# Two pool places fewer for the expert tokens, float32 pieces at the end, and another way to the last norm

## The chip, the cores and the metric

The kernel runs on one core of a Trainium2 chip. TensorE (PE), VectorE (DVE), ScalarE (ACT), GpSimd (POOL) and SyncE (SP) run their own instruction queues; weights come from HBM by DMA. The metric is the device time of one launch in microseconds (us); lower is better.

## The reference

Two layers act on 256 tokens of width 1024, all in float32. In each, two mixers (windowed attention and a gated delta rule) are merged and added, and a channel mixer follows: a dense SwiGLU in layer 0, eight experts with the top two per token in layer 1. After each half comes a layer norm. The part that the change touches:

```
def moe_swiglu(x, router_w, w_gate, w_up, w_down):
    logits = x @ router_w
    top_val, top_idx = lax.top_k(logits, TOP_K)
    top_w = softmax(top_val)
    gates = sum(one_hot(top_idx, 8) * top_w)        # (tokens, experts)
    y = 0
    for e in range(8):
        y += gates[:, e] * ((silu(x @ w_gate[e]) * (x @ w_up[e])) @ w_down[e])
    return y                                        # w_gate, w_up: 1024 x 3584; w_down: 3584 x 1024
x = layer_norm(alpha * x + moe_swiglu(x, ...), ln2_g, ln2_b)
```

## The kernel before, in words

**Splitting.** Float32 products are built from halves: `hi` is a rounded copy of a value and `lo` the rest, and x·w is taken as hi·hi + hi·lo + lo·hi, three matmuls per 128 rows of depth.

**The stream of weights.** Every weight piece is 128 partitions x 1024 float32 (512 KB) and comes by one DMA on SP's queue (L145) into a tile `raw`. `Stream.advance` splits it: ACT casts `raw` to `whi` (L165), DVE subtracts to get `wlo` (L167). TensorE then uses the pair (`use`) and gives it back (`retire`). Two caps, set in the code by `caps(raw, spl)`, say how many pieces the program splits ahead of TensorE and how many more it loads ahead of these. Pieces marked "plain" are used in float32 as they lie in `raw`, with no cast and no subtraction.

**The pool.** `raw`, `whi`, `wlo`, and the experts' tokens come from one pool with a single tag (`k4`): 36 places of 4 KB per partition, given out in a ring. A tile that needs a place waits until the last reader of the tile that had it before is done. So a long-lived tile in the ring makes the ring shorter for all the others.

**The experts.** `moe` (L1593) runs over the eight experts, ranked by how many tokens they have, in eight stages, i = 0 to 7. Four stages (i = 1, 3, 5, 7) are "narrow": 64 slots, with hi and lo side by side as the 128 columns of the stationary operand, so two matmuls per 128 rows of depth (`packed`, L1543 and L1544). The others are "wide": 128 slots, three matmuls in gate and up (`gemm`, L473 to L475), and plain float32 down pieces (`unsplit`, L1557). A stage has seven chunks of 512 hidden columns; each chunk is four gate pieces (`mg`), four up pieces (`mu`) and four down pieces of the rank before (`oe`, `md` in the code). The hidden values pass ACT and DVE (`mgs`, L1455 to L1467), are transposed by TensorE (`ht`, L1481) and copied back as `htp` or `htn`. After a rank's last chunk, `scatter` scales its output into `oh` and `ol` (L1500, L1501), multiplies by the placement matrix (`sc`, L1507, L1508) and adds to `x` (L1511).

**The gather.** `route` (from L1260) keeps the tokens as `xnh` and `xnl`, hi and lo, two of each: four places of the pool to the end of the kernel. `gather(i)` builds the tokens of the next two ranks (`xe` wide, `xen` narrow) with four matmuls (L1394) in each of eight steps. It starts in the third chunk of an even i.

**The order.** The big matmuls are a main line; `tick` runs background chains (hidden, scatter, gather) a step at a time between them, and `lag(n)` keeps a chain back for n steps so that TensorE doesn't reach an instruction before its input is ready. `as_written` then fixes the order of PE, DVE and ACT as the program wrote it.

**The end.** The last rank's down pieces run one half of the output columns after the other (f = 0, then f = 1), seven chunks of two pieces each, all split. Then `overflow` (an If that all engines pass, L1649; not taken here), two DMAs on SP that spread the norm's g and b to all partitions (`ln_params`, L1134), and `last_norm`: statistics, then per half of 512 columns an ACT scaling, a DVE product and an addition on DVE or POOL (L1634 to L1636).

Of the kernel before, what the change touches and what calls it, by code (L numbers as in the profile page):

```python
# [187 lines left out]
class Kern:  # L188
# [234 lines left out]
    def plan(self):  # L423
# [18 lines left out]
        def add(nm, r, c, j):  # L442
            W.add((nm, r, c, j), [piece(r, i) for i in moe_pieces(nm, c, j)], 512, nm == "md" and self.plain(r))
        for i, r in enumerate(RANKS):
# [10 lines left out]

    def plain(self, r):

        return r not in NARROW

# [799 lines left out]
    def route(self):  # L1259
# [19 lines left out]
        sel = self.small([P, 2, 8], "sel", 1, BF16)  # L1279
        self.xn = [[], []]  # L1280
        for t in range(2):
            lg = yield from self.narrow(rp, 8, "lg", t)
            nc.vector.max(mx[:, t], lg)
            nc.vector.max_index(mi[:, t], mx[:, t], lg)
            nc.vector.tensor_copy(ix[:, t], mi[:, t, :2])
            nc.vector.tensor_scalar(first[:, t], io8, ix[:, t, 0:1], None, op0=OP.is_equal)
            nc.vector.scalar_tensor_tensor(sel[:, t], io8, ix[:, t, 1:2], first[:, t], op0=OP.is_equal, op1=OP.add)
            yield
            hi = self.k4([P, D], F32R, name="xnh")
            lo = self.k4([P, D], F32R, name="xnl")  # L1290
            nc.scalar.copy(hi, self.x[t])
            nc.vector.tensor_tensor(lo, self.x[t], f32(hi), op=OP.subtract)
            self.xn[0].append(hi)
            self.xn[1].append(lo)
        ps = self.bg("rank")
# [79 lines left out]
    def gather(self, i):  # L1375
# [13 lines left out]
        for d in range(8):  # L1389
            yield from self.take()  # L1390
            ps = self.bg("xe")
            for j in range(2):
                for t in range(2):
                    nc.tensor.matmul(ps[:, j * n:(j + 1) * n], lhsT=self.xn[j][t][:, d * P:(d + 1) * P],  # L1394
                                     rhs=self.Pt[i][:, t].rearrange("p e c -> p (e c)")[:, c0:c1],
                                     start=(t == 0), stop=(t == 1))
# [96 lines left out]
    def scatter(self, e, f, oe):  # L1493
# [7 lines left out]
        nc.vector.scalar_tensor_tensor(lo, oe, gs, f32(hi), op0=OP.mult, op1=OP.subtract)  # L1501
        self.flags.add(("oh", e, f))
        yield
        for t in range(2):
# [10 lines left out]
    def down(self, r, c, fs=(0, 1)):  # L1515
# [10 lines left out]
        for f in fs:  # L1526
            keys, ends = [(("md", r, c, f), 0)], dict(first=(c == 0), last=(c == 6))
            if r in NARROW:
                yield from self.packed(keys, self.oe[f], lambda k: ht[:, k], **ends)
            else:  # L1530
                yield from self.unsplit(keys, self.oe[f], lambda k: ht[:, k], **ends)
            if c == 6:
                self.add_chain(self.scatter(r, f, self.oe[f]), ("scat", r, f), 1)
# [59 lines left out]
    def moe(self):  # L1593
        nc = self.nc
        self.Pt, self.xe, self.PT, self.ht = {}, {}, {}, {}
        self.taken = False
        self.add_chain(self.route(), ("route",), 1)
        self.dense()
        first = len(self.traced())
        for i, r in enumerate(RANKS):  # L1600
            self.add_chain(self.slots(r), ("slots", r), 1)
            for c in range(0 if i else 1, 7):
                if i % 2 == 0 and c == 2 and i < NE - 1:
                    self.add_chain(self.gather(i // 2 + 1), ("gather", i // 2 + 1), 1)
                if c == 0 and i % 2 == 1:
                    self.finish([("gather", i // 2 + 1)])
                res = {}

                def go(nm):
# [4 lines left out]
                if i:  # L1614
                    self.run(self.down(RANKS[i - 1], c))
        for f in range(2):
            for c in range(7):
                self.run(self.down(RANKS[-1], c, (f,)))
        self.finish([("scat", r, f) for r in range(NE) for f in range(2)])
        self.as_written(first)  # L1620
        self.overflow()
        g2, b2 = self.ln_params(2, 1, nc.sync)
        self.last_norm(g2, b2)

    def last_norm(self, g, b):
        nc = self.nc
        mv = [self.norm_stats(t, LN_EPS) for t in range(2)]
        for t in range(2):
            x = self.x[t]
            nb = self.small([P, 1], "nb", 2)  # L1630
            nc.vector.scalar_tensor_tensor(nb, mv[t][:, 0:1], -1.0, mv[t][:, 3:4], op0=OP.mult, op1=OP.mult)
            for h in range(2):
                s = slice(h * 512, (h + 1) * 512)
                nc.scalar.activation(x[:, s], x[:, s], AF.Identity, bias=nb, scale=mv[t][:, 3:4])  # L1634
                nc.vector.tensor_tensor(x[:, s], x[:, s], g[:, s], op=OP.mult)  # L1635
                (nc.vector if h else nc.gpsimd).tensor_tensor(x[:, s], x[:, s], b[:, s], op=OP.add)  # L1636
                nc.sync.dma_start(self.out[0, t * P:(t + 1) * P, s], x[:, s])

    def overflow(self):
# [9 lines left out]
        with tc.If(n > 0):  # L1649
            with tc.For_i(0, NE, 1) as e:  # L1650
# [16 lines left out]
                for d in range(8):  # L1667
                    ps = self.bg("xe")
                    for j in range(2):
                        for t in range(2):  # L1670
                            nc.tensor.matmul(ps[:, :P], lhsT=f32(self.xn[j][t])[:, d * P:(d + 1) * P], rhs=p2[:, t],
                                             start=(j == 0 and t == 0), stop=(j == 1 and t == 1))
                    nc.vector.tensor_copy(xe[:, d], ps[:, :P])
# [43 lines left out]
    def build(self):  # L1717
# [8 lines left out]
        self.CAP_MOE0 = (12, 5)  # L1726
        self.CAP_MOE = (14, 5)
        self.LAG = 9
        with ExitStack() as es:
# [55 lines left out]
```

## Time and profile before

| | |
|---|---|
| median of 3 runs | 1896.44 us (1896.32 to 1897.02) |
| the profiled execution | 1896.58 us, span 1894.8 us |
| PE busy | 1844.7 us, 97% of the span |
| DVE busy | 1459.6 us, 77% |
| ACT busy | 1164.2 us, 61% |
| split subtractions on DVE (L167) | 838, mean 1215 ns |
| split casts on ACT (L165) | 838, mean 1047 ns |
| DMA | 513.50 MB, mean 271 GB/s, 400 and more in many slices of the expert part |

The expert part lies between about 950 and 1878 us. In 40 slices of the span PE is at nine tenths or more in nearly all. A matmul group's busy time is modelled with a pipelined end, so that neighbours overlap: the distance of two starts is the better price. "Idle" in brackets behind a row is the time for which the engine stood before it, and what released it.

### The profile page before, as it was taken

To read this page: it belongs to the slowest core of one execution; us is meant where nothing else is said; L and a number is where in the kernel's file an instruction comes from. 1 tells how busy PE (TensorE), PEld (TensorE's weight loads), DVE (VectorE), ACT (ScalarE), POOL (GpSimd) and SP (SyncE) were. 2 spreads that over 40 slices of the span, in tenths; PEclk is the share of its full clock that TensorE was granted. 3 is DMA by queue.
4 is the path that set the end of the run, shared out by engine and by line. 5 is a ranking of instruction groups with operands and counts; after the bars stand their busy time and mean duration, and the time that the engine had idled before them with its cause. 6 is when DMAs were issued, how large, how long until landed. Compare 5 with 4: busy or idle time off the path is not lost. (4 is left out here: it accounts for less than half of the span.)

```text
span 1894.8 us, 27869 instructions
## 1 busy us (share of the span) xinstructions
PE 1844.7 (97%) x9279; PEld 1466.0 (77%) x9279; DVE 1459.6 (77%) x2147; ACT 1164.2 (61%) x1710; POOL 163.0 (9%) x221
## 2 busy tenths in 40 slices
PE   8999999999999999999999999999999999999995
PEld 7998888888889998888878766886678766787663
DVE  7888666675556887757588878998788977989777
ACT  6664555454444754545357767786678866787673
POOL 2113202000001212201220000000000000000000
PEclk9999999999999999999999999999999999999997
DMA  9445343674655445444749999999999999999992
GB/s 322 140 147 179 134 150 115 203 242 147 196 200 191 142 137 189 135 147 145 252 159 335 384 409 408 366 395 391 410 400 365 402 394 409 396 372 409 409 409 107
DMA packets 154374, 513.50 MB, mean 271 GB/s; under 512 B 26320, under 2 KB 28592, under 8 KB 154224
## 3 DMA queue, kind: packets, MB, share of 16 engines
q1 hardware_dynamic: 151984, 504.10, 72.1%
q0 software_dynamic: 2240, 7.56, 1.2%
q8 instruction: 75, 1.23, 0.3%
q14 instruction: 75, 0.61, 0.1%
HBM read 506.09 MB, written 5.51 MB: 270 GB/s over the span
## 5 line engine op out<-in xcount | busy, mean ns | idle before, releaser
L167 DVE TENSOR_TENSOR wlo<-raw,whi 128x1024 fp32r<-128x1024 f32 (+1 forms) x838 | 997.3, 1215 | 219.2 <-ACT whi L165 175.2
L165 ACT CAST whi<-raw 128x1024 fp32r<-128x1024 f32 x838 | 849.7, 1047 | 238.0 <-PE oe L1557 63.6
L1557 PE MATMUL oe<-raw,htp 128*128 128x512 f32 x448 | 197.5, 592 | 0.0
L1557 PEld LDWEIGHTS oe<-raw,htp 128*128 128x128 f32 x448 | 84.7, 190 | 94.6 <-issue 91.9
L627 PE MATMUL qb<-xhl,whi 128*128 128x256 f32 x384 | 110.4, 288 | 0.0
L632 PE MATMUL qb<-xhl,wlo 128*128 128x256 f32 x384 | 108.9, 283 | 0.6 <-DVE wlo L167 0.6
L630 PE MATMUL qb<-xhl,whi 128*128 128x256 f32 x384 | 108.5, 283 | 0.0
L473 PE MATMUL at<-whi,xhl 128*128 128x512 f32 x256 | 106.8, 417 | 0.0
L475 PE MATMUL at<-whi,xhl 128*128 128x512 f32 x256 | 101.2, 395 | 0.0
L474 PE MATMUL at<-wlo,xhl 128*128 128x512 f32 x256 | 100.8, 394 | 0.0
L1543 PE MATMUL mg<-whi,xen 128*128 128x512 f32 x224 | 97.4, 435 | 0.0
L1115 POOL TENSOR_TENSOR bnmv<-bnmv,mhalf 128x1 f32<-128x1 f32 x8 | 7.0, 871 | 1006.6 <-DVE bnmv L1114 1006.6
L1543 PE MATMUL mu<-whi,xen 128*128 128x512 f32 x224 | 91.5, 409 | 0.0
L1544 PE MATMUL oe<-wlo,htn 128*128 128x512 f32 x224 | 89.6, 400 | 0.9 <-DVE wlo L167 0.9
L1543 PE MATMUL oe<-whi,htn 128*128 128x512 f32 x224 | 89.6, 400 | 0.0
L1544 PE MATMUL mu<-wlo,xen 128*128 128x512 f32 x224 | 88.7, 396 | 0.0
L1544 PE MATMUL mg<-wlo,xen 128*128 128x512 f32 x224 | 87.8, 392 | 0.0
L473 PE MATMUL mg<-whi,xe 128*128 128x512 f32 x216 | 87.7, 406 | 0.0
L475 PE MATMUL mg<-whi,xe 128*128 128x512 f32 x216 | 85.2, 394 | 0.0
L473 PE MATMUL mu<-whi,xe 128*128 128x512 f32 x216 | 85.1, 394 | 0.0
L474 PE MATMUL mg<-wlo,xe 128*128 128x512 f32 x216 | 84.9, 393 | 0.0
L475 PE MATMUL mu<-whi,xe 128*128 128x512 f32 x216 | 84.3, 390 | 0.0
(456 smaller groups left out, 3817.5 us busy)
## 6 DMA issues: line engine op xcount, KB each, us to landing
raw<-in_moe SPq DMA_DIRECT2D x672, 512.0 KB
raw<-in_trunk SPq DMA_DIRECT2D x270, 512.0 KB
lx<-LT SPq DMA_DIRECT2D x8, 256.0 KB
Dm<-dx SPq DMA_DIRECT2D x8, 256.0 KB
raw<-in_trunk SPq DMA_DIRECT2D x8, 256.0 KB
lng<-in_ln_g POOLq DMA_DIRECT2D x3, 512.0 KB, 5.8
lnb<-in_ln_b POOLq DMA_DIRECT2D x3, 512.0 KB, 8.0
dx<-zero POOLq DMA_DIRECT2D x4, 256.0 KB, 5.0
```

The lines of the kernel that those rows point to most:

```text
L165: k.last_act = nc.scalar.copy(hi[:, :, :n], raw[:, :, :n])
L167: ins = (nc.gpsimd if share and a else nc.vector).tensor_tensor(lo[:, a:b, :n], r[:, :, :n], f32(hi)[:, a:b, :n], op=OP.subtract)
L473: nc.tensor.matmul(o, lhsT=xh, rhs=hi[:, kk, :n], start=st, stop=False)
L474: nc.tensor.matmul(o, lhsT=xh, rhs=lo[:, kk, :n], start=False, stop=False)
L475: mm = nc.tensor.matmul(o, lhsT=xl, rhs=hi[:, kk, :n], start=False, stop=en)
L627: nc.tensor.matmul(o, lhsT=hi[:, kk, w], rhs=self.xhl[k // 2][:, k % 2, :S], start=(k == 0 and b % 2 == 0), stop=False, skip_group_check=True)
L630: nc.tensor.matmul(o, lhsT=hi[:, kk, w], rhs=self.xhl[k // 2][:, k % 2, S:], start=False, stop=False, skip_group_check=True)
L632: self.dense_pe = nc.tensor.matmul(o, lhsT=lo[:, kk, w], rhs=self.xhl[k // 2][:, k % 2, :S], start=False, stop=(k == 7), skip_group_check= ...
L1115: nc.gpsimd.tensor_tensor(mv[:, 3:4], mv[:, 2:3], self.mhalf[:, 0:1], op=OP.pow)
L1543: nc.tensor.matmul(o, lhsT=x(k0 + kk), rhs=hi[:, kk], start=first and i == 0 and kk == 0, stop=False)
L1544: nc.tensor.matmul(o, lhsT=x(k0 + kk), rhs=lo[:, kk], start=False, stop=last and end)
L1557: nc.tensor.matmul(o, lhsT=x(k0 + kk), rhs=w[:, kk], start=first and i == 0 and kk == 0, stop=last and end)
```

## The change

1. `route` keeps the tokens once, in float32 (`xs`): two places instead of four. Each gather step casts its 128 x 256 piece to `xsh` on ACT and subtracts to `xsl` on DVE before its four matmuls. They use the tags `cth` and `cy` of another pool, three places each; two of `cy` hold the rows of the last norm to the end.
2. In the last rank's second half (f = 1) the pieces of chunks 3 to 6, eight pieces, are plain float32, used by `unsplit`.
3. The caps are (8, 5) from the last gate and up chunk on, and (6, 8) for the last down pieces.
4. The scatter of the last rank's first half is kept back six more steps.
5. `norm_rows` loads g and b early as hi and lo rows; after the If eight matmuls spread them over the partitions into PSUM. `last_norm` takes the statistics of x[0] on DVE and of x[1] on ACT, and does all scaling in DVE instructions that read PSUM.

```diff
--- before.py
+++ after.py
@@ -440,7 +440,7 @@
             return src
         def add(nm, r, c, j):
-            W.add((nm, r, c, j), [piece(r, i) for i in moe_pieces(nm, c, j)], 512, nm == "md" and self.plain(r))
+            W.add((nm, r, c, j), [piece(r, i) for i in moe_pieces(nm, c, j)], 512, nm == "md" and self.plain(r, c, j))
         for i, r in enumerate(RANKS):
             for c in range(7):
                 for nm in ("mg", "mu"):
@@ -453,9 +453,10 @@
             for c in range(7):
                 add("md", RANKS[-1], c, f)
-    def plain(self, r):
-        return r not in NARROW
+    def plain(self, r, c=0, f=0):
+        return r not in NARROW or (r == RANKS[-1] and f == 1 and c > 2)
     def gemm(self, keys, accs, x, first=True, last=True, tiles=(0, 1)):
@@ -1277,7 +1278,8 @@
         ix = self.small([P, 2, 2], "ix")
         first = self.small([P, 2, 8], "first")
         sel = self.small([P, 2, 8], "sel", 1, BF16)
-        self.xn = [[], []]
+        self.xs = [self.k4([P, 2, 512], name="xs") for _ in range(2)]
         for t in range(2):
             lg = yield from self.narrow(rp, 8, "lg", t)
             nc.vector.max(mx[:, t], lg)
@@ -1286,12 +1288,8 @@
             nc.vector.tensor_scalar(first[:, t], io8, ix[:, t, 0:1], None, op0=OP.is_equal)
             nc.vector.scalar_tensor_tensor(sel[:, t], io8, ix[:, t, 1:2], first[:, t], op0=OP.is_equal, op1=OP.add)
             yield
-            hi = self.k4([P, D], F32R, name="xnh")
-            lo = self.k4([P, D], F32R, name="xnl")
-            nc.scalar.copy(hi, self.x[t])
-            nc.vector.tensor_tensor(lo, self.x[t], f32(hi), op=OP.subtract)
-            self.xn[0].append(hi)
-            self.xn[1].append(lo)
+            for h in range(2):
+                nc.scalar.copy(self.xs[h][:, t], self.x[t][:, h * 512:(h + 1) * 512])
         ps = self.bg("rank")
         nc.tensor.matmul(ps[:, 0:8], lhsT=self.triS, rhs=sel[:, 0], start=True, stop=True)
         nc.tensor.matmul(ps[:, 8:16], lhsT=self.ones16, rhs=sel[:, 0], start=True, stop=False)
@@ -1388,10 +1386,15 @@
         n = c1 - c0
         for d in range(8):
             yield from self.take()
+            x = self.xs[d // 4][:, :, d % 4 * P:(d % 4 + 1) * P]
+            xp = [self.mp.tile([P, S], F32R, name=nm, tag=tag, bufs=3).rearrange("p (t c) -> p t c", t=2)
+                  for nm, tag in (("xsh", "cth"), ("xsl", "cy"))]
+            nc.scalar.copy(xp[0], x)
+            nc.vector.tensor_tensor(xp[1], x, f32(xp[0]), op=OP.subtract)
             ps = self.bg("xe")
             for j in range(2):
                 for t in range(2):
-                    nc.tensor.matmul(ps[:, j * n:(j + 1) * n], lhsT=self.xn[j][t][:, d * P:(d + 1) * P],
+                    nc.tensor.matmul(ps[:, j * n:(j + 1) * n], lhsT=xp[j][:, t],
                                      rhs=self.Pt[i][:, t].rearrange("p e c -> p (e c)")[:, c0:c1],
                                      start=(t == 0), stop=(t == 1))
             v = ps[:, :2 * n].rearrange("p (j c) -> p j c", j=2)
@@ -1500,6 +1503,8 @@
         nc.scalar.activation(hi, oe, AF.Copy, scale=gs)
         nc.vector.scalar_tensor_tensor(lo, oe, gs, f32(hi), op0=OP.mult, op1=OP.subtract)
         self.flags.add(("oh", e, f))
+        if e == RANKS[-1] and f == 0:
+            yield from self.lag(6)
         yield
         for t in range(2):
             yield from self.take()
@@ -1525,7 +1530,9 @@
         ht = self.ht[r, c]
         for f in fs:
             keys, ends = [(("md", r, c, f), 0)], dict(first=(c == 0), last=(c == 6))
-            if r in NARROW:
+            if r in NARROW and self.plain(r, c, f):
+                yield from self.unsplit(keys, self.oe[f], lambda k: f32(ht)[:, k], **ends)
+            elif r in NARROW:
                 yield from self.packed(keys, self.oe[f], lambda k: ht[:, k], **ends)
             else:
                 yield from self.unsplit(keys, self.oe[f], lambda k: ht[:, k], **ends)
@@ -1594,6 +1601,7 @@
         nc = self.nc
         self.Pt, self.xe, self.PT, self.ht = {}, {}, {}, {}
         self.taken = False
+        self.norm_rows()
         self.add_chain(self.route(), ("route",), 1)
         self.dense()
         first = len(self.traced())
@@ -1605,6 +1613,9 @@
                 if c == 0 and i % 2 == 1:
                     self.finish([("gather", i // 2 + 1)])
                 res = {}
+                if (i, c) == (NE - 1, 6):
+                    self.W.caps(*self.CAP_END[0])
                 def go(nm):
                     res[nm] = yield from self.expert(r, c, nm)
@@ -1613,28 +1624,76 @@
                 self.run(go("mu"))
                 if i:
                     self.run(self.down(RANKS[i - 1], c))
+        self.W.caps(*self.CAP_END[1])
         for f in range(2):
             for c in range(7):
                 self.run(self.down(RANKS[-1], c, (f,)))
         self.finish([("scat", r, f) for r in range(NE) for f in range(2)])
         self.as_written(first)
         self.overflow()
-        g2, b2 = self.ln_params(2, 1, nc.sync)
-        self.last_norm(g2, b2)
-    def last_norm(self, g, b):
-        nc = self.nc
-        mv = [self.norm_stats(t, LN_EPS) for t in range(2)]
-        for t in range(2):
-            x = self.x[t]
-            nb = self.small([P, 1], "nb", 2)
-            nc.vector.scalar_tensor_tensor(nb, mv[t][:, 0:1], -1.0, mv[t][:, 3:4], op0=OP.mult, op1=OP.mult)
+        first = len(self.traced())
+        self.last_norm()
+        self.as_written(first)
+    def norm_rows(self):
+        nc = self.nc
+        H = 64
+        self.sel = self.small([H, 4], "lnsel", 1, F32R)
+        nc.vector.tensor_tensor(self.sel, self.ident[:H, :4], self.ident[:H, 32:36], op=OP.add)
+        self.rows = []
+        for s in "gb":
+            raw = self.mp.tile([P, S], F32, name="lnraw", tag="cth", bufs=3)[:H]
+            row = self.mp.tile([P, S], F32R, name="lnrow", tag="cy", bufs=3)[:H]
+            nc.gpsimd.memset(raw, 0.0)
+            for p in (0, 32):
+                nc.gpsimd.dma_start(raw[p:p + 4], self.A[f"ln2_{s}"][1].rearrange("(r n) -> r n", r=4))
+            nc.scalar.copy(row, raw)
+            nc.vector.tensor_tensor(row[32:], raw[32:], f32(row)[32:], op=OP.subtract)
+            self.rows.append(row)
+    def last_norm(self):
+        nc = self.nc
+        sc = [self.acc("lng") for _ in range(2)] + [self.acc("lnb") for _ in range(2)]
+        for r in range(8):
+            nc.tensor.matmul(sc[r // 2][:, r % 2 * S:(r % 2 + 1) * S],
+                             lhsT=self.sel[:, r % 4:r % 4 + 1].to_broadcast([64, P]), rhs=self.rows[r // 4], start=True,
+                             stop=True)
+        st = self.small([P, 2, 2], "lnst")
+        nm = self.small([P, 4], "lnnm")
+        junk = self.k2([P, 512], name="lnj")
+        h_ = [slice(h * 512, (h + 1) * 512) for h in range(2)]
+        x = self.x[1]
+        for h, s in enumerate(h_):
+            nc.scalar.activation(junk, x[:, s], AF.Identity, accum_out=st[:, 0, h:h + 1])
+        mv = self.norm_stats(0, LN_EPS)
+        def scaled(t, h):
+            x = self.x[t][:, h_[h]]
+            nc.vector.scalar_tensor_tensor(x, x, (mv if t == 0 else nm)[:, 0:1], sc[h], op0=OP.subtract, op1=OP.mult)
+        def shifted(t, h):
+            x = self.x[t][:, h_[h]]
+            nc.vector.scalar_tensor_tensor(x, x, mv[:, 3:4] if t == 0 else nm[:, 3:4], sc[2 + h], op0=OP.mult, op1=OP.add)
+            nc.sync.dma_start(self.out[0, t * P:(t + 1) * P, h_[h]], x)
+        scaled(0, 0)
+        scaled(0, 1)
+        nc.vector.tensor_tensor(nm[:, 0:1], st[:, 0, 0:1], st[:, 0, 1:2], op=OP.add)
+        nc.vector.tensor_scalar(nm[:, 0:1], nm[:, 0:1], 1.0 / D, None, op0=OP.mult)
+        nc.vector.tensor_scalar(nm[:, 1:2], nm[:, 0:1], -1.0, None, op0=OP.mult)
+        for h, s in enumerate(h_):
+            nc.scalar.activation(junk, x[:, s], AF.Square, bias=nm[:, 1:2], accum_out=st[:, 1, h:h + 1])
+        shifted(0, 0)
+        shifted(0, 1)
+        nc.vector.tensor_tensor(nm[:, 2:3], st[:, 1, 0:1], st[:, 1, 1:2], op=OP.add)
+        nc.vector.tensor_scalar(nm[:, 2:3], nm[:, 2:3], 1.0 / D, LN_EPS, op0=OP.mult, op1=OP.add)
+        nc.gpsimd.tensor_tensor(nm[:, 3:4], nm[:, 2:3], self.mhalf[:, 0:1], op=OP.pow)
+        for f in (scaled, shifted):
             for h in range(2):
-                s = slice(h * 512, (h + 1) * 512)
-                nc.scalar.activation(x[:, s], x[:, s], AF.Identity, bias=nb, scale=mv[t][:, 3:4])
-                nc.vector.tensor_tensor(x[:, s], x[:, s], g[:, s], op=OP.mult)
-                (nc.vector if h else nc.gpsimd).tensor_tensor(x[:, s], x[:, s], b[:, s], op=OP.add)
-                nc.sync.dma_start(self.out[0, t * P:(t + 1) * P, s], x[:, s])
+                f(1, h)
     def overflow(self):
...
@@ -1725,6 +1783,7 @@
         self.CAP_WO1 = (9, 10)
         self.CAP_MOE0 = (12, 5)
         self.CAP_MOE = (14, 5)
+        self.CAP_END = ((8, 5), (6, 8))
         self.LAG = 9
         with ExitStack() as es:
             self.cp = es.enter_context(tc.tile_pool(name="consts", bufs=1))
```

Three places show how the order moves. The first is VectorE at the end of the kernel, from the last rank's `oh`/`ol` on; `wlo` are the subtractions of weight pieces, `x` the additions of scattered output. Before:

```order
L1501 SCALAR_TENSOR_TENSOR ol<-oe,gs,oh 128x512 x2
L167 TENSOR_TENSOR wlo<-raw,whi 128x1024 x3
L1511 TENSOR_TENSOR x_9315<-x_9315,sc 128x512
L167 TENSOR_TENSOR wlo<-raw,whi 128x1024
L1490 TENSOR_TENSOR htn<-ht,htn 128x4x64
L167 TENSOR_TENSOR wlo<-raw,whi 128x1024 x4
L1511 TENSOR_TENSOR x_9315<-x_9315,sc 128x512
L167 TENSOR_TENSOR wlo<-raw,whi 128x1024 x5
L1511 TENSOR_TENSOR x_9316<-x_9316,sc 128x512
L167 TENSOR_TENSOR wlo<-raw,whi 128x1024 x4
L1511 TENSOR_TENSOR x_9316<-x_9316,sc 128x512
L167 TENSOR_TENSOR wlo<-raw,whi 128x1024 x2
```

After these come one `ol`, five more subtractions, and the last additions. After the change:

```order
L1504 SCALAR_TENSOR_TENSOR ol<-oe,gs,oh 128x512 x2
L167 TENSOR_TENSOR wlo<-raw,whi 128x1024 x6
L1516 TENSOR_TENSOR x_9315<-x_9315,sc 128x512
L167 TENSOR_TENSOR wlo<-raw,whi 128x1024
L1493 TENSOR_TENSOR htn<-ht,htn 128x4x64
L167 TENSOR_TENSOR wlo<-raw,whi 128x1024 x4
L1516 TENSOR_TENSOR x_9315<-x_9315,sc 128x512
L167 TENSOR_TENSOR wlo<-raw,whi 128x1024 x5
L1516 TENSOR_TENSOR x_9316<-x_9316,sc 128x512 x2
L1504 SCALAR_TENSOR_TENSOR ol<-oe,gs,oh 128x512
```

The 24 subtractions are 16, and the `ol` of the first half stands behind all of them.

The second is TensorE at the same place, the last down pieces (`oe`) and scatters (`sc`). Before, from the last scatter but one on, where split pieces alternate to the end:

```order
L1507 MATMUL sc<-oh,PT 128x512
L1508 MATMUL sc<-ol,PT 128x512
L1543 MATMUL oe<-whi,htn 128x512
L1544 MATMUL oe<-wlo,htn 128x512
L1543 MATMUL oe<-whi,htn 128x512
L1544 MATMUL oe<-wlo,htn 128x512
```

After the change:

```order
L1550 MATMUL oe<-whi,htn 128x512
L1551 MATMUL oe<-wlo,htn 128x512
L1564 MATMUL oe<-raw,htn 128x512 x5
L1512 MATMUL sc<-oh,PT 128x512
L1513 MATMUL sc<-ol,PT 128x512
L1564 MATMUL oe<-raw,htn 128x512 x10
L1512 MATMUL sc<-oh,PT 128x512
L1513 MATMUL sc<-ol,PT 128x512
L1564 MATMUL oe<-raw,htn 128x512
```

Sixteen float32 matmuls stand where 32 split ones stood, and both scatters of the first half lie among them.

The third is VectorE in the first stage of the expert part, where the first gather of the loop runs; `Pt` is the placement matrix. Before:

```order
L1372 TENSOR_SCALAR Pt<-ioL,rkr 128x128 x2
L1372 TENSOR_SCALAR Pt<-ioP,rkr 128x128 x2
L167 TENSOR_TENSOR wlo<-raw,whi 128x1024 x5
L1467 TENSOR_TENSOR mgs<-mgs,mu 128x512
L167 TENSOR_TENSOR wlo<-raw,whi 128x1024 x8
```

After the change:

```order
L1370 TENSOR_SCALAR Pt<-ioL,rkr 128x128 x2
L1370 TENSOR_SCALAR Pt<-ioP,rkr 128x128 x2
L1393 TENSOR_TENSOR xsl<-xs,xsh 128x256
L167 TENSOR_TENSOR wlo<-raw,whi 128x1024 x3
L1393 TENSOR_TENSOR xsl<-xs,xsh 128x256
L167 TENSOR_TENSOR wlo<-raw,whi 128x1024 x2
L1470 TENSOR_TENSOR mgs<-mgs,mu 128x512
L167 TENSOR_TENSOR wlo<-raw,whi 128x1024 x2
L1393 TENSOR_TENSOR xsl<-xs,xsh 128x256
```

The subtractions of the tokens stand between those of the weight pieces, one after every two to four.

## Rows read from the trace of the kernel before

**Rows 1.** Waits of TensorE, 940 to 1880 us: line, releaser, total, times, longest

```profile
PE ht L1481 <- DVE mgs L1467: 9.9, 19, 1.1
```

**Rows 2.** Windows: stretch, length, busy by engine, granted clock, DMA share, GB/s

```profile
1070.00:1180.00 110.00, 106.67 (x381) 67.77 (x380) 84.12 (x88) 72.71 (x88) 0.00 (x0) 1.00 1.03 409
1250.00:1280.00 30.00, 30.00 (x138) 24.87 (x137) 29.11 (x27) 26.09 (x29) 0.00 (x0) 1.00 1.03 408
1280.00:1290.00 10.00, 8.02 (x30) 6.06 (x30) 10.00 (x11) 7.45 (x10) 0.00 (x0) 0.83 1.02 407
1740.00:1835.00 95.00, 95.00 (x335) 59.24 (x334) 75.60 (x82) 62.55 (x77) 0.00 (x0) 1.00 1.03 409
1863.80:1869.50 5.70, 5.70 (x14) 4.46 (x15) 5.70 (x6) 0.00 (x0) 0.00 (x0) 0.50 0.00 0
```

**Rows 3.** Timeline of TensorE, starts of chunks: start, length, instruction

```profile
1280.28 0.39 PE L1543 MATMUL mg<-whi,xen 128*128 128x512 f32 x1
...
1316.04 0.80 PE L1543 MATMUL mg<-whi,xen 128*128 128x512 f32 x1
...
1392.26 0.79 PE L473 MATMUL mg<-whi,xe 128*128 128x512 f32 x1
...
1729.32 0.39 PE L1543 MATMUL mg<-whi,xen 128*128 128x512 f32 x1
...
1762.64 0.80 PE L1543 MATMUL mg<-whi,xen 128*128 128x512 f32 x1
...
1821.66 0.79 PE L1543 MATMUL mg<-whi,xen 128*128 128x512 f32 x1
```

**Rows 4.** Waits in 1290 to 1400 us, stage i=3

```profile
ACT whi L165 <- PE oe L1557: 16.8, 8, 3.4
...
DVE wlo L167 <- DMA raw<-in_moe: 4.0, 4, 1.4
```

**Rows 5.** Timeline of TensorE at the border to i=3

```profile
1284.75 0.63 PE L1481 MATMUL ht<-ident,mgs 128*128 128x128 f32 x4 [1.13 <-DVE mgs L1467]
...
1286.45 0.80 PE L1508 MATMUL sc<-ol,PT 128*128 128x512 f32 x1 [0.85 <-DVE ol L1501]
```

**Rows 6.** Timeline of ACT, then DVE, in the gather of i=2

```profile
1209.16 1.05 ACT L165 CAST whi<-raw 128x1024 fp32r<-128x1024 f32 x1 [0.78 <-PE mu L474]
...
1210.24 2.59 DVE L167 TENSOR_TENSOR wlo<-raw,whi 128x1024 fp32r<-128x1024 f32 x2 [1.12 <-ACT whi L165]
```

**Rows 7.** The gather's matmuls of i=2: shortest, median, longest ns, first and last start

```profile
L1394 PE MATMUL xe<-Pt,xnh x16: 277/280/365, 1205.5 to 1240.2; 128*128 128x256 f32 x16
```

**Rows 8.** Timeline of DVE in the last down pieces

```profile
1838.67 3.50 DVE L167 TENSOR_TENSOR wlo<-raw,whi 128x1024 fp32r<-128x1024 f32 x3 [0.18 <-ACT whi L165]
...
1843.82 0.41 DVE L1490 TENSOR_TENSOR htn<-ht,htn 128x256 fp32r<-128x256 f32 x1
...
1862.97 0.74 DVE L1501 SCALAR_TENSOR_TENSOR ol<-oe,gs,oh 128x512 fp32r<-128x512 f32 x1
```

**Rows 9.** Timeline of TensorE, float32 down pieces: two records for each matmul

```profile
1084.02 7.03 PE L1557 MATMUL oe<-raw,htp 128*128 128x512 f32 x16
```

**Rows 10.** Timeline of TensorE at the end

```profile
1863.77 0.80 PE L1508 MATMUL sc<-ol,PT 128*128 128x512 f32 x1 [3.93 <-DVE ol L1501]
...
1874.80 0.39 PE L1543 MATMUL oe<-whi,htn 128*128 128x512 f32 x1
1875.03 0.39 PE L1544 MATMUL oe<-wlo,htn 128*128 128x512 f32 x1
...
1877.55 0.40 PE L1508 MATMUL sc<-ol,PT 128*128 128x512 f32 x1
```

**Rows 11.** The chain that ended last, in order of time: start, length, work

```profile
1881.51 3.96 DMA lng<-in_ln_g
...
1889.88 1.64 DVE x L1636
```

**Rows 12.** Waits of SP's queue, 1850 to 1895 us

```profile
SPq L1134 <- PEq L1649: 22.7, 1, 22.7
```

More of the change, by code (lines that the diff above doesn't have):

```diff
@@ L1668, in overflow @@
                     ps = self.bg("xe")
[L1669 to L1672, printed above, removed]
+                    for t in range(2):
+                        nc.tensor.matmul(ps[:, :P], lhsT=self.xs[d // 4][:, t, d % 4 * P:(d % 4 + 1) * P], rhs=p2[:, t],
+                                         start=(t == 0), stop=(t == 1))
                     nc.vector.tensor_copy(xe[:, d], ps[:, :P])
```

## The prediction

> **What bounds the kernel now.** I read the waits of TensorE first, then the busy times by stage, then the starts of the chunks, and the tail instruction by instruction. Over the whole expert part TensorE waits little; the longest sum is 9.9 us in 19 pieces at the transposes `ht`, for the DVE product `mgs` [rows 1]. Yet the stages are unlike. In narrow stages TensorE works 106.67 of 110 us, in the last one 95.00 of 95, and DMA moves 409 GB/s in both [rows 2]. The reader should look at where chunks start [rows 3]: the narrow stage i=3 takes from 1316.04 to 1392.26 us for its last five chunks, 15.24 us each; the stage i=7, whose matmuls are the same, takes from 1762.64 to 1821.66 for four, 14.76 each. Its first two chunks need 33.32 us (1729.32 to 1762.64), those of i=3 need 35.76 (1280.28 to 1316.04). What differs is the pool: at i=7 no further `xe` is being held, so the same 36 places are shared by fewer tiles. How a lack of places reaches TensorE is seen in the waits of i=3: the cast of a weight piece waits 16.8 us for TensorE to give a place back [rows 4], the subtraction after it is late, and the DVE product behind that in the queue is late for `ht`. So the expert part is bound by TensorE with about half a microsecond per narrow chunk lost to places; the end is bound by other things, taken below.
>
> **Two places of the pool.** The normed tokens' four 4 KB tiles become two, so 36 places lose two holders for the rest of the kernel. In my reading of the two orders, stages i=3 and i=5 then have what i=7 has now. I take the full difference for the steady chunks: 15.24 − 14.76 = 0.48 us, five chunks in each of i=1, 3, 5, so 15 × 0.48 = 7.2 us. As a check, it cannot exceed the 9.9 us idle at `ht` [rows 1]. Bounds: 0 (below) and 9.9.
>
> **The wide-to-narrow borders.** [...] At i=7 the same two chunks are 35.76 − 33.32 = 2.44 us shorter. There are two such borders (i=3 and 5), 4.9 us if both become like i=7. But DVE is busy 29.11 of the 30 us before a border [rows 2] and i=7 also follows a lighter stage, so I take 60%: 2.9 us. Bounds 0 and 4.9.
>
> **The split in the gather.** Each of 40 gather steps gets an ACT cast and a DVE subtraction of 128x256; only four large pairs (two casts, two subtractions of 128x1024) go. A DVE subtraction of 128x256 lasts 0.41 us [rows 8], so eight steps are 3.3 us of DVE per gather. The order shows the danger: `xsl` has one place, and stands on DVE behind the subtraction of the piece four ahead of TensorE's. A split takes 1.05 us of cast and about 1.3 of subtraction after TensorE released its place (the cast starts at 1209.16, the subtractions at 1210.24, two in 2.59) [rows 6], 2.4 us in all; TensorE spends six matmuls of 0.23 (1874.80 to 1875.03) [rows 10], 1.4 us, on a wide piece. With a place given back one piece earlier there is about a piece of slack more than now, and 0.4 to 0.8 us (a cast and a subtraction of 0.4 each, together or one beside other work) are asked of it. I take 0.06 us for each of 32 steps, 2 us, and 1 us for the first gather at the head of the expert part, where tokens are split while TensorE has little else: 3.0 us lost. Bounds: 0, and 32 × 0.8 = 26 us where each step pays cast and subtraction in full (the rival below).
>
> [...]
>
> **The float32 down pieces.** Eight of the last 24 subtractions go. DVE runs without rest from 1838.67: a subtraction every 1.17 (3.50 for three) [rows 8], and the scatter at 1863.77 had waited 3.93 us for `ol` [rows 10], which stands at 1862.97 behind the subtractions; afterwards 14 matmuls run at half clock in 5.70 us [rows 2]. After the change DVE has 16 subtractions, one `htn` and two adds ahead of its last piece's end: 1838.67 + 16 × 1.17 + 0.41 + 2 × 0.74 (an add taken like `ol`) = 1859.3. One piece of four matmuls follows, 0.9 us, then 16 float32 matmuls. A float32 matmul leaves two records, 16 of them in 7.03 us [rows 9], so 0.88 each: 14.1 us where 32 split ones took 7.4. With two scatter pairs of 0.46 the last down matmul ends at 1875.2, against 1875.42 now (1875.03 + 0.39). The scatter after it is unchanged and ends at 1877.95 (1877.55 + 0.40) [rows 10]. Gain 0.2 us. If TensorE is never held by DVE it needs, from 1837.8 on, 20 pieces of 0.92, 14.1 and four scatter pairs, to 1872.1: a gain of 3.3. If the float32 part falls to half clock for as long as the split ones do now, it is a loss of 2.6. I take a gain of 0.8, near the first: DVE governs, and with more places it may start a little earlier. The smaller caps at the end make DMA later by a few pieces of 1.28 us (512 KB at 409 GB/s); those pieces are used some 15 us after they land, which hides it.
>
> **The last norm.** Now SP's load of `lng` is issued at 1881.51, lands 3.96 later, and the last DVE write starts at 1889.88 and takes 1.64, to 1891.52 [rows 11]. After: no load; eight small matmuls behind the If put g and b into PSUM. SP had waited 22.7 us at the If for TensorE's sequencer [rows 12], which left it about 1881.5, 3.5 us after its last matmul (1877.95). I let the new matmuls start there, 0.5 us to the first half, and then DVE has eight instructions of 512 columns that read PSUM (`ol` is one: 0.74 [rows 8]) and about five small ones of 0.15: 1882.0 + 5.9 + 0.8 = 1888.7. Gain 2.8 us. Bounds: 0.7 (each as slow as 1.0) and 4.5 (matmuls ready when the statistics are).
>
> [...] The trace shows 3.5 us between TensorE's last matmul and its leaving the If, so I stay with the row.
>
> **Sum.** 7.2 + 2.9 − 3.0 + 0.8 + 2.8 = 10.7 us. The profiled execution took 1896.58 us, its span 1894.8 and 1.8 around it; it stands 0.14 above the median of the runs. 1896.58 − 10.7 = 1885.9, from the median 1885.7, which I say.
>
> **The rivals.**
> - *The narrow stages are bound by DMA.* Twelve pieces at 409 GB/s are 15.36 us, and the chunk of i=3 takes 15.24; there DVE waited 4.0 us for pieces that had not landed [rows 4]. Then the places give nothing in the middle nor at the borders: −3.0 + 0.8 + 2.8 = 0.6, so 1895.8, no change. Against it: i=7 runs its chunks in 14.76 at the same 409 GB/s, from pieces that came ahead, and in wide stages the queue has room to come ahead again.
> - *The gather stalls TensorE: slower.* If at each of the 32 steps in wide stages `xsl` comes after TensorE wants it, by cast plus subtraction (0.8 us), this costs 26 us, and 1 at the first gather, against 13.7 of gains: 1909.7. The gains are gone from 0.40 us a step on. For it: one place for `xsl`, and DVE 97% busy before the borders. Against: eight steps (two records of each kind) lie between 1205.5 and 1240.2, about 5 us apart [rows 7], and the gather is over before the fullest stretch.
> - *All of it works.* The borders become like i=7 in full, the tail is not held by DVE, and the gather costs only its first 1 us: 7.2 + 4.9 − 1.0 + 3.3 + 2.8 = 17.2, so 1879.2.
> - *Half of it:* the places go to raw pieces, and only half the steady and border gain comes: 3.6 + 1.5 − 3.0 + 0.8 + 2.8 = 5.7, so 1890.7.
>
> **Chances.** My forecast 0.45, half of it 0.15, all of it 0.12, DMA-bound 0.14, gather stall 0.14. What the measurement can tell is 0.2%, 3.8 us: faster means below 1892.6, slower above 1900.2. The first three are faster (0.72, less 0.02 for the edge), the DMA case lies within, the gather case mostly above: 0.70, 0.16, 0.14. The range from 1877 to 1896.5 leaves out the gather case and a little below. The likeliest case alone spans 1881 to 1890.
>
> **What would show it.** In the profile after: chunks of i=3 and i=5 at 14.76 us and no waits of `ht` on `mgs` there; the clock not falling at the borders; the waits of TensorE at the `xe` matmuls for `xsl` summing to some 2 us; `ol` of the last rank's first half no longer waited for 4 us; the first write of the last norm about a microsecond after TensorE leaves the If, and no load there. Chunks still at 15.2 us would prove the pool the wrong cause; waits of half a microsecond or more at every `xe` step would make the time slower.

## The result, and the profile after

The changed kernel takes 1882.36 us (median of five, 1880.11 to 1887.23) against 1896.44: 0.9931 of the time before, interval 0.9917 to 0.9945, so 14.1 us faster by the medians. The forecast of 1885.7 had the sign and, within 3.3 us, the size. The profiled execution took 1881.69 us, span 1879.9, 14.9 less than the one before. Two executions, one of 3080.51 us without the float32 end and one of 4746.87 us of the kernel before, lie far from all others and are left out of every median and ratio below.

Four of TensorE's waits in the whole kernel; `lng` and `xe` are new, the other two smaller than before (line, releaser, total us, times, longest):

```profile
PE lng L1662 <- PEq L1708: 3.2, 1, 3.2
PE xe L1397 <- DVE xsl L1393: 2.7, 4, 1.7
PE sc L1513 <- DVE ol L1504: 2.6, 4, 0.8
...
PE ht L1484 <- DVE mgs L1470: 1.6, 3, 0.6
```

The 9.9 us at `ht` [rows 1] are 1.6. The starts of the same chunks as in [rows 3], on TensorE's timeline:

```profile
1280.71 0.39 PE L1550 MATMUL mg<-whi,xen 128*128 128x512 f32 x1
...
1314.09 0.80 PE L1550 MATMUL mg<-whi,xen 128*128 128x512 f32 x1
...
1387.83 0.79 PE L474 MATMUL mg<-whi,xe 128*128 128x512 f32 x1
...
1719.71 0.39 PE L1550 MATMUL mg<-whi,xen 128*128 128x512 f32 x1
...
1752.02 0.80 PE L1550 MATMUL mg<-whi,xen 128*128 128x512 f32 x1
...
1811.02 0.79 PE L1550 MATMUL mg<-whi,xen 128*128 128x512 f32 x1
```

Stage i=3 now runs its last five chunks in 14.75 us each (73.74 / 5), as i=7 does (59.00 / 4), and its first two in 33.38 instead of 35.76. The border before it, and the window there (length, busy by engine, granted clock, DMA share, GB/s):

```profile
1284.62 0.63 PE L1484 MATMUL ht<-ident,mgs 128*128 128x128 f32 x4 [0.57 <-DVE mgs L1470]
...
1286.32 0.50 PE L1513 MATMUL sc<-ol,PT 128*128 128x512 f32 x1 [0.85 <-DVE ol L1504]
```

```profile
1280.00:1290.00 10.00, 8.58 (x39) 6.61 (x38) 10.00 (x12) 9.18 (x12) 0.00 (x0) 1.00 1.02 408
```

Half of the first wait is gone, the second is as before [rows 5], and the clock no longer falls: 1.00 where it was 0.83 [rows 2]. At the end, DVE first, then TensorE:

```profile
1848.92 0.74 DVE L1504 SCALAR_TENSOR_TENSOR ol<-oe,gs,oh 128x512 fp32r<-128x512 f32 x1
```

```profile
1853.18 0.39 PE L1513 MATMUL sc<-ol,PT 128*128 128x512 f32 x1
...
1865.61 0.40 PE L1513 MATMUL sc<-ol,PT 128*128 128x512 f32 x1
...
1869.20 1.19 PE L1662 MATMUL lng<-lnrow,lnsel 64*128 64x256 f32 x4 [3.19 <-PEq L1708]
```

`ol` is done at 1849.66, 3.5 us before its matmul starts, where TensorE had waited 3.93 us for it [rows 10]. In the last norm, DVE:

```profile
1870.00 1.41 DVE L1676 SCALAR_TENSOR_TENSOR x<-x,bnmv,lng 128x512 f32<-128x512 f32 x2 [0.90 <-PE lng L1662]
...
1875.22 1.40 DVE L1680 SCALAR_TENSOR_TENSOR x<-x,lnnm,lnb 128x512 f32<-128x512 f32 x2
```

From the start of the last `sc` to the last write it is 11.0 us (1865.61 to 1876.62); before it was 14.0 (1877.55 to 1891.52).

One place got worse, the head of the expert part. From its first gate matmul (948.53 before, 949.14 after) to the start of i=1 (1059.98, 1063.90) it takes 114.8 us instead of 111.4. Here TensorE, DVE and POOL in the first gather:

```profile
976.83 0.44 PE L1397 MATMUL xe<-Pt,xsl 128*128 128x128 f32 x2 [1.74 <-DVE xsl L1393]
```

```profile
971.50 1.51 DVE L1393 TENSOR_TENSOR xsl<-xs,xsh 128x256 fp32r<-128x256 f32 x1
972.93 1.78 DVE L167 TENSOR_TENSOR wlo<-raw,whi 128x512 fp32r<-128x512 f32 x1
...
975.23 1.21 DVE L167 TENSOR_TENSOR wlo<-raw,whi 128x1024 fp32r<-128x1024 f32 x1
976.37 0.41 DVE L1393 TENSOR_TENSOR xsl<-xs,xsh 128x256 fp32r<-128x256 f32 x1
```

```profile
970.93 3.23 POOL L167 TENSOR_TENSOR wlo<-raw,whi 128x512 fp32r<-128x512 f32 x2 [7.04 <-ACT whi L165]
```

The `xsl` that TensorE waits 1.74 us for is the one at 976.37. It stands on DVE behind weight subtractions, two instructions of that queue having taken 1.51 and 1.78 us while POOL worked.

The account by stretches of the two spans: 0.6 lost ahead of the expert part (where its start varies from 947.8 to 951.4 us over the kernels below), 3.3 lost in its head, 14.6 won from the start of i=1 to the last chunk of i=7 (761.7 to 747.1 us; "the middle" below), 4.2 won from there to the end (73.1 to 68.9).

### The profile page after: what moved, and what is told of

It reads as the page before. It is cut to its first block, busy times and chain, and to the rows that moved or that the text cites. A ratio compares the mean times of both kernels' runs of the same rounds, so it can differ in the third digit from the quotient of the medians.

```text
span 1879.9 us, 27958 instructions
## 1 busy us (share of the span) xinstructions
PE 1846.6 (98%) x9287; PEld 1464.8 (78%) x9287; DVE 1461.0 (78%) x2181; ACT 1167.0 (62%) x1750; POOL 160.2 (9%) x225
## 5 line engine op out<-in xcount | busy, mean ns | idle before, releaser
L475 PE MATMUL mu<-wlo,xe 128*128 128x512 f32 x216 | 84.2, 390 | 0.0
L1550 PE MATMUL oe<-whi,htn 128*128 128x512 f32 x208 | 81.8, 393 | 0.0
```

The source lines that it names most:

```text
L475: nc.tensor.matmul(o, lhsT=xh, rhs=lo[:, kk, :n], start=False, stop=False)
L1550: nc.tensor.matmul(o, lhsT=x(k0 + kk), rhs=hi[:, kk], start=first and i == 0 and kk == 0, stop=False)
```

## The experiments

Times are medians beside the kernel before on the same chip; "middle" and "head" are of the one profiled execution. The rival that mattered was whether the pool's places are the cause at all.

**34 places.** `self.n4 = 34` in the changed kernel.

> The changed kernel with a pool of 34 places instead of 36; nothing else. Theory (places): the gain of the middle, 14.6 us from the start of stage i=1 to the last chunk of i=7, goes away: narrow chunks 15.2 us instead of 14.75, first two chunks of i=3 and i=5 35.8 instead of 33.4, waits of ht on mgs near 10 us; about 1897 us. Rival (another order, the caps or the split in the gather bring the gain, or DMA sets the narrow chunks): chunks stay at 14.75 and the time within 2 us of the changed kernel's 1882.

1906.5 us, ratio 1.005 (1.0036 to 1.0065). The chunks and the waits at `ht` went back; and the time went 9.5 us past the 1897 that was expected. In the middle the gather now stalls. Waits from 1060 to 1850 us:

```profile
PE ht L1484 <- DVE mgs L1470: 9.9, 19, 1.1
PE xe L1397 <- DVE xsl L1393: 3.9, 8, 0.7
```

The chunk of i=2 in which most of the gather lies:

```profile
1228.36 0.40 PE L474 MATMUL mg<-whi,xe 128*128 128x512 f32 x1
...
1248.01 0.39 PE L474 MATMUL mg<-whi,xe 128*128 128x512 f32 x1
```

It takes 19.65 us, against 17.59 in the changed kernel and 16.99 before. The middle is 768.6 us, 6.9 more than before. The head is 118.7 us, 7.2 more than before, with two falls of the granted clock (0.78 in 980 to 985 us, 0.58 in 995 to 1000). So the slower rival had a point, in part: with two places fewer the split does stall TensorE, by 3.9 us in 8 waits and not by 0.8 us at each of 32 steps, and it is the freed places that pay for it.

**The float32 end left out.** All pieces of the last expert split, caps (14, 5) to the end, no `lag(6)`.

> The changed kernel with all down pieces of the last expert split again, the caps left at (14, 5) to the end, and no six steps more before the scatter; the two pool places and the new norm stay. Theory: the wait for ol of about 4 us and the half clock after it are back, 1.4 us lost: about 1883.8 us. Rival (the float32 end brings nothing, or brings the second group of times near 1887): 1882 or less, and all runs within 2 us of each other.

1883.92 us, ratio 0.9930 (0.9917 to 0.9943), five times from 1880.9 to 1887.5. The wait of 3.9 us for `ol` is back, and the stretch from the last chunk to the end is 69.8 instead of 68.9. The float32 end is worth 0.9 us by these two traces, which the times can't tell from nothing; the spread isn't its doing.

**The tokens alone.** Part 1 of the change, with old end and old norm.

> The kernel before with the tokens kept once and split in the gather, and neither the float32 end nor the new norm. Theory (the places bring 14.6, the first gather loses 3.3 and 0.7 ahead of it): 10.5 us faster than the kernel before, about 1886. Rival (the parts help each other; alone the places bring the 7 us of the steady chunks): about 1892.

1881.88 us, ratio 0.9924 (0.9911 to 0.9937): as fast as the whole change, where 1886 was expected. Middle 747.2. Four executions lie at 1881.3 to 1882.2; the profiled one is the fifth, 1888.06, and shows what such an execution has (windows of this kernel, then of the changed one):

```profile
990.00:995.00 5.00, 4.16 (x12) 3.40 (x13) 4.69 (x15) 0.00 (x0) 0.00 (x0) 0.59 0.14 33
995.00:1000.00 5.00, 5.00 (x26) 4.54 (x25) 3.38 (x5) 2.26 (x3) 0.00 (x0) 0.72 0.98 388
```

```profile
990.00:995.00 5.00, 4.38 (x28) 4.00 (x29) 4.76 (x13) 2.02 (x3) 0.00 (x0) 1.00 0.26 80
995.00:1000.00 5.00, 5.00 (x23) 4.13 (x22) 5.00 (x7) 3.90 (x6) 0.00 (x0) 1.00 0.92 348
```

After the same waits (1.67 and 0.64 us at `PT`, later in the head) the granted clock fell here, to 0.59 in 990 to 995 us, and stayed at 1.00 there; the first chunk after takes 19.2 instead of 16.1 us. Two of the changed kernel's five executions lie near 1887. Their mean granted clock is 0.992, as in this execution, against 0.995 and 0.996 in the other three, so more of them ran at the lower clock. Neither was profiled: that it fell at the same place stays likely and not shown.

**The norm alone.** Part 5 on the kernel before.

> The kernel before with the new last norm and its early rows, nothing else. Theory: 3.0 us between the last scatter and the last write, so 1893.5 us; chunks as before. Rival (the early rows cost the expert part's start as much): 1896, no change.

1893.11 us, ratio 0.9983 (0.9973 to 0.9993). As expected; chunks as before.

**The float32 end alone.** Parts 2 to 4 on the kernel before.

> The kernel before with the eight float32 down pieces, the smaller caps at the end and the six steps more before the scatter; tokens and norm as before. Theory: the wait of 3.9 us for ol and the half clock behind it go, the float32 matmuls cost most of it again: 1.4 us faster, about 1894.8. Rival (DVE keeps TensorE waiting, or the last pieces come late with the smaller caps): 1896 or more, with waits of oe or sc over 2 us in the tail.

1895.17 us, ratio 0.9994 (0.9983 to 1.0005). No wait of `ol` over 0.8 us is left, and last chunk to end is 72.1 us instead of 73.1: the wait is gone as meant, the size is under what the times resolve.

**Fewer pieces loaded ahead.** `CAP_MOE = (12, 5)` for (14, 5) in the changed kernel.

> The changed kernel with the cap on pieces loaded ahead of the split 12 instead of 14 in the expert part. Tells which of the two leads the freed places feed. Theory S (the places let a piece be split earlier; DMA has lead to spare): narrow chunks stay at 14.75, time within 2 us of 1882. Rival D (they let DMA run further ahead, which the narrow stages live on): narrow chunks lengthen towards 15.2 and the time rises by 5 us or more.

1880.71 us, ratio 0.9926 (0.9913 to 0.9939). Neither theory foresaw a gain, and the trace has one: the middle falls by another 4.3 us, to 742.8, all waits at `ht` are gone and the `sc` waits there are 1.2 us. The head of this execution is 118.0 us, with two falls of the granted clock (0.69 in 975 to 980 us, 0.55 in 990 to 995), so the time hides it. The waits from 1060 to 1820 us:

```profile
PE sc L1513 <- DVE ol L1504: 1.2, 2, 0.6
```

The ring of 36 was not only short: 14 pieces waiting unsplit filled it.

**Every token subtraction twice.** `for _ in range(2):` before the subtraction to `xsl`.

> The changed kernel with every subtraction of the gather made twice into the same tile, so each of the 40 steps asks 0.33 us more of DVE. Theory (a piece of slack, 1.4 us, is there in the wide stages and 0.4 of it is used): chunks of i=2, 4, 6 lengthen by less than 0.2 us in all, only the first gather loses 1 to 2 us; about 1883.5. Rival (the gather is at its limit): TensorE waits at xe grow by 0.33 us a step, 32 steps, about 10 us: 1892.

1887.41 us, ratio 0.9963 (0.9950 to 0.9976). Middle 750.3, head 115.9. The 3.1 us lost in the middle lie between the two expectations: the chunk with most of a gather goes from 17.59 to 18.63 in i=2 and by as much in i=4, the others move by some 0.3 us or less. TensorE's waits from 1060 to 1850 us, where the changed kernel has 0.5 us:

```profile
PE xe L1398 <- DVE xsl L1394: 2.0, 4, 0.7
```

So the slack is used up in one chunk of these two gathers, and hardly in the rest; my piece of slack at every step was too much.

**The first gather from early halves.** In `route`, `xnh` and `xnl` as before and `xs` beside them; `gather` takes `self.xn` where `i == 0`, else splits.

> The changed kernel, but the first gather takes its hi and lo from whole tiles made in route, as before the change; these four places are given back after that gather, and the later gathers split from the float32 copy. Theory (the 3.3 us lost at the head of the expert part come from the split inside the first gather, and the group of times near 1887 from the clock falling there after waits for xsl): head as before, 111.4 us to the start of i=1 instead of 114.8, no waits of xe there, about 1879 us, and no second group. Rival (the four more places of that time delay the weights): head as long as now, 1882.

1879.40 us, ratio 0.9919 (0.9906 to 0.9931), all six between 1878.1 and 1881.7. TensorE's waits in the head, none of them at `xe`:

```profile
PE PT L1432 <- DVE gtr L1340: 2.3, 2, 1.7
PE tp L283 <- issue: 1.9, 1, 1.9
```

The head is 113.3 us in an execution where the granted clock fell twice in it (0.72 in 955 to 960 us, 0.79 in 985 to 990); kernels with the old tokens have 111.4 to 111.5 us with one such fall (0.66 in 985 to 990 in the kernel before) and 112.5 to 112.9 with two (0.66 in 955 to 960 and 0.73 in 985 to 990 with cap 10). So most of the loss at the head was the split inside the first gather, some half a microsecond is left unexplained, and the group near 1887 did not occur.

**The kernel before with one number changed.** `CAP_MOE = (12, 5)`; no other edit.

> The kernel before with one number changed: the cap on pieces loaded ahead of the split is 12 instead of 14 in the expert part. Theory (what the change gave to the middle is two places for the split pieces, whoever frees them): from the start of i=1 to the last chunk of i=7 about 747 us instead of 761.7, no waits of ht on mgs, head as before; about 1882 us. Rival (the narrow stages live on pieces loaded ahead): chunks of 15.2 us or longer, 1896 us or more.

1881.89 us, ratio 0.9924 (0.9910 to 0.9937): the whole gain of the change. Middle 745.9; the waits at `ht` are 1.5 us, as in the changed kernel. i=3 from its third chunk to the end, 14.75 us a chunk:

```profile
1308.91 0.80 PE L1543 MATMUL mg<-whi,xen 128*128 128x512 f32 x1
...
1382.68 0.79 PE L473 MATMUL mg<-whi,xe 128*128 128x512 f32 x1
```

**And with 10.**

> The kernel before with that cap at 10. Theory: two places more for the split pieces, as the changed kernel had with 12: about 743 us from i=1 to the last chunk, 1878 us. Rival (loading ahead becomes too short): TensorE or ACT wait for raw in the narrow stages, chunks longer than 14.75, time above that of cap 12.

1878.67 us, ratio 0.9910 (0.9895 to 0.9925). Middle 742.5. The rival's sign appears without its price. Waits in i=3, 1290 to 1400 us:

```profile
ACT whi L165 <- DMA raw<-in_moe: 9.9, 4, 3.3
ACT whi L165 <- PE oe L1557: 8.3, 5, 2.2
```

ACT now waits for loads as well, and half as long for these places as before (16.8 us, [rows 4]); TensorE waits for neither.

**Both mends on the changed kernel.** Early halves for the first gather, and cap 12.

> The changed kernel with the first gather from early hi and lo and the cap on loaded pieces 12. Theory: the two gains add, 111.4 us of head and 743 of middle: about 1875 us, faster than every kernel so far. Rival (the head needs the pieces loaded ahead): no better than 1879.

1875.47 us, ratio 0.9887 (0.9872 to 0.9902): head 113.2, middle 742.8. The lowest median of all, and faster than both kernels of the case.

**The old tokens with cap 10, the new end and norm.**

> The kernel before with the float32 end and the new norm of the change, the tokens in four places as before, and the cap on loaded pieces 10. Theory (the cap does what the two places do, without the split in the gather): the time with cap 10 alone, 1878.7, less 3.0 for the norm and 1.4 for the end: about 1874.3, a microsecond under the best so far. Rival (the places given back by the change are needed beside the early rows and the end's caps): 1877 or more.

1876.50 us, ratio 0.9893 (0.9876 to 0.9909), between theory and rival and not to be told from the one above. Head 111.4 and middle 743.0 are as expected. In the profiled execution, what is missing lies behind the If, where TensorE stands between the first and second `lng` matmul for a reason that the trace does not name:

```profile
1864.13 1.00 PE L1660 MATMUL lng<-lnrow,lnsel 64*128 64x256 f32 x3 [2.43 <-issue]
```

## Why the prediction was right, point by point

**Steady narrow chunks: right.** Forecast 7.2 us; i=3 alone gives 76.22 − 73.74 = 2.5, i=1, 3 and 5 together 7.3. The 34 places take it back. What I called a lack of places is more exactly a division of them: the cap of 14 let unsplit pieces hold what the split pieces lacked, as caps 12 and 10 on the kernel before show. To that extent the rival by which places go to raw pieces was real: with cap 12 the changed kernel's middle falls by another 4.3 us. That stage i=7 showed what two free places would do was the reading that carried the forecast. The path that I gave, a cast that waits for a place and a DVE product that comes late behind it, is seen in the kernel before:

```profile
1363.06 1.05 ACT L165 CAST whi<-raw 128x1024 fp32r<-128x1024 f32 x1 [1.37 <-PE mg L1543]
1364.15 1.23 DVE L167 TENSOR_TENSOR wlo<-raw,whi 128x1024 fp32r<-128x1024 f32 x1 [1.20 <-ACT whi L165]
1366.00 0.68 DVE L1467 TENSOR_TENSOR mgs<-mgs,mus 64x512 f32<-64x512 f32 x1
1366.74 0.46 PE L1481 MATMUL ht<-ident,mgs 64*128 64x64 f32 x4 [0.31 <-DVE mgs L1467]
```

In the same chunk of the changed kernel `mgs` is done at 1361.53, 1.4 us before TensorE wants it:

```profile
1360.85 0.68 DVE L1470 TENSOR_TENSOR mgs<-mgs,mus 64x512 f32<-64x512 f32 x1
...
1362.93 0.46 PE L1484 MATMUL ht<-ident,mgs 64*128 64x64 f32 x4
```

But the sum of 16.8 us that I pointed at [rows 4] does not measure the lack. From 1290 to 1400 us in the changed kernel ACT waits nearly as long for these places, with no wait at `ht` left in the last five chunks of i=3:

```profile
ACT whi L165 <- PE oe L1564: 15.5, 7, 4.6
```

**Borders: mechanism right, mis-sized.** I took 60% of 4.9 us, in doubt whether DVE before the border would let it. Both borders came to i=7's level in full (2.4 and 2.5 us), i=7 won another 1.0, and the granted clock did not fall: 1.00 in 1280 to 1290 us, where it was 0.83 in the kernel before [rows 2], with waits of 1.13 and 0.85 us [rows 5]. The wide stages and the first two chunks of i=1 gave some 1.3 more, net of the gather, which was in no term.

**Gather in the wide stages: right in sign, too dear.** Forecast −2.0; the two chunks with most of a gather, in i=2 and i=4, lost 0.6 us each. The price of a small subtraction was right: median 0.42 us in 40, against 0.41. The reason I gave, a piece of slack at each step, fell with the doubled subtraction: one chunk of the gathers in i=2 and i=4 is at its limit. The rival's stall appears with two places fewer, at a fraction of its price.

**First gather: mis-sized.** Forecast −1.0, "where tokens are split while TensorE has little else"; measured −3.3, and up to 8 in an execution where the granted clock fell as well (0.81 in 980 to 985 us, 0.60 in 995 to 1000; head 119.4 us in the kernel without the float32 end). There TensorE has the dense product's matmuls to do, and the eight steps come about 1.9 us apart (968.98 to 982.33), where they were about 5 apart in the loop [rows 7]. Early halves show it: no waits at `xe`.

**Float32 end: the wait went, a gain in time is not shown.** Forecast +0.8 us; the trace gives 1.3 from the last chunk to the last scatter (55.9 to 54.6), and 0.9 to the end beside the kernel without it. But the tokens alone and the norm alone, whose last pieces are all split and whose TensorE waits the same 3.9 us for `ol`, have 54.6 and 54.4 in their traces. In the ten microseconds around and after that scatter their granted clock is 0.83 (1857 to 1867 and 1864 to 1874 us), and 0.66 in the kernel before (1863 to 1873). So the 1.3 us go with a lower clock in one profiled execution, and where the clock fell less the float32 end had nothing to win.

**Norm: right.** Forecast +2.8; measured 3.0, by the trace and by the medians with the norm alone. TensorE left the If 3.19 us after its last matmul, where I had read 3.5 from the trace of before. DVE then waited 0.90 us for `lng`, so the matmuls were not ready when the statistics were, and the gain of 4.5 in that case did not come.

**The rival of DMA as the bound: refuted.** Chunks of 14.75 at the same 409 GB/s in i=3, 5 and 7 refute it, and with less loaded ahead the kernel got faster.

**The sum: near, in part by luck.** By the two spans the borders with i=7 gave 5.9 us for 2.9, and the wide stages with i=1 won 1.3 where the gather was to lose 2.0; the first gather lost 3.3 for 1.0. The total is as near as it is because these errors partly cancel, and the 1882.4 measured lies midway between the forecast and the case in which all of it works (1879.2).

The parts don't add by their times: alone they are worth 14.2 (tokens), 3.0 (norm) and 2.1 us (float32 end, not clear of zero) by medians, together 14.1. The tokens alone leave `xsl` three places of its tag, since no `lnrow` holds two. In the traces the first chunk of the head, which holds the first gather, is 36.1 us there against 37.7 in the changed kernel, with one fall of the granted clock in each (0.66 and 0.79 in 960 to 965 us); so the place that `xsl` lacks may account for some 1.6 us. The rest stays open.

## What to carry to other kernels

When one ring of buffers serves several stages of a pipeline, read which stage waits for a place before freeing places: here the loads held them and the splits lacked them, and lowering one cap did what two freed places did, without new work. A stage of the same kernel that happens to have the resource spare is the best forecast of what freeing it brings. The work that was moved in front of the gather's matmuls here was cheap where the program ran pieces ahead (0.6 us in the chunk with most of a gather, in i=2 and i=4), and dear at the start, before it did (3.3 us in the head).

## What the runs showed of the hardware

- A DVE subtraction of 128x256, median 0.42 us in the 40 of the gather, took 1.51 us while POOL did two subtractions of 128x512 (3.23 us). In the old norm, too, a DVE sum of 128x512 that started during POOL's (1889.88) took 1.64 us; one that started just ahead of POOL's (1886.89) took 0.69.
- The granted clock fell after some waits of TensorE and not after equal ones in another execution: at the head, with the same 1.67 and 0.64 us, it was 0.59 from 990 to 995 us with the tokens alone and 1.00 in the changed kernel. In the kernel before, a wait of 1.13 and one of 0.85 us close together were followed by a fall at both borders (0.66 in 1285 to 1290 us and in 1510 to 1515); in the changed kernel 0.57 and 0.85 at the first of them were not (1.00 in 1280 to 1290).
